# Reading order, weight interleaving and start addresses of the gate and up matmuls in a hybrid decoder layer

## The chip, the cores and the metric

The kernel runs on one core of a Trainium2 chip. The metric is device time in microseconds, from the first to the last instruction of one execution with what the launch adds around it. The engines are named as in the profile: PE is TensorE's matmuls, PEld its weight loads, DVE is VectorE, ACT is ScalarE, POOL is GpSimd, SP is SyncE. "Pitch" or "spacing" of matmuls means the distance between the starts of two that follow each other.

## The reference

One decoder layer on 512 tokens of width 2048 with 16 learned meta tokens ahead of them, all in float32:

```python
n = rmsnorm(h, g_mix)
q, k, v, gb, gc, u = split(n @ w_in)          # attention: 8 heads x 128; convolution: 1024 channels
o_attn = stick_breaking_attention(norm(q), norm(k), v)
o_conv = gb * causal_dwconv(gc * u, conv_w)
h = h + concat(rmsnorm(o_attn), rmsnorm(o_conv)) @ w_out
n2 = rmsnorm(h, g_ffn)
h = h + (silu(n2 @ w_gate) * (n2 @ w_up)) @ w_down    # hidden width 5632
return h[:, 16:]
```

The change touches only the two products `n2 @ w_gate` and `n2 @ w_up`.

## The kernel before, in words

**Number format.** Each float32 operand is held as a high part, rounded to the matmul's own format (fp32r), and a low part, the rest. A product takes three matmuls: high x high, high x low, low x high. Each of them loads a 128x128 block of weights and moves 256 columns (tokens) past it.

**Blocks and pairs.** The FFN works on pairs. Gate and up of one hidden tile f (128 of the 5632 hidden units, so there are FT = 44 tiles) form one pair: two matrices of 2048 x 128, each cut in two quarters of 1024 rows, against activations cut in two halves of the rows and two halves of the tokens. By a scheme with seven products in place of eight (`pair_product`, L900 to 945) the pair is computed from seven `block_product`s (L871 to 891). Each takes one sum of weight quarters and one sum of activation blocks, and accumulates into one of three banks of PSUM, x, y or z. A block product of gate and up has 8 blocks of 128 rows and three matmuls for each, so 24 matmuls, and a pair has 168.

**Weights.** A quarter is 128 partitions x 1024 columns of float32, and comes in by one transfer from `w_gu` (`load_quad`, L168, on SP's queue). On the host (L1388) the quarter is laid out so that its 8 blocks of 128 columns lie side by side in a partition; block k is columns 128k to 128k+127. DVE adds quarters (`add_quads`, L213, and L278), ACT makes the high part (L203), DVE the low part (L206) in one of three places of `sw_split`, ahead of TensorE by two block products (`prepare`, L235; `next_w`, L304, keeps the distance). The pieces go in the order of the list `pieces` (L145 to 150); `pairs[i]` with CONV <= i < CONV + FT are the gate and up pairs.

**Activations.** The seven activation blocks f0 to f6 stay in SBUF for all 44 pairs. Each is a tile of 128 partitions with a high and a low part, of 8 row blocks and 256 tokens each. `slots` (L1017) makes them: it asks for 64 elements more than it needs and starts the block 4 elements (16 bytes) into the tile. In the allocation of this kernel each of these tiles begins at 224 modulo 256 bytes, so every block begins at 240, and as its parts and row blocks are multiples of 1024 bytes, so does every moving operand. The same helper makes the `ring` and `first` tiles of the down projection, which begin at 240 too. Blocks f3, f0, f1, f2, f5 are allocated at L1028, f6 and f4 at L1094 to 1096; f4 and f6 are loaded back from DRAM, the others are written by `split_f` (L1116) in the output projection.

**The matmul itself.** In `block_product` the slice `kk` (L885) picks 128 neighbouring columns of the weights, `ah` and `al` are 256 neighbouring tokens, and `p` 256 neighbouring columns of the bank. The three matmuls are L887 (high x high), L890 (high x low) and L891 (low x high). The convolution's pairs go through the same lines with activations from the tiles `n` and `mixed`, whose blocks begin at other places, and the down projection with those of `first` and `ring`.

**Around it.** After a pair DVE and ACT scale, apply silu, multiply gate and up and split the result (`gate`, L1217); POOL stores it to DRAM (L1206), from where the down projection loads it.

Of the kernel before, what the change touches and what calls it, by code (L numbers as in the profile page):

```python
# [10 lines left out]
F32R = mybir.dt.float32r  # L11
# [4 lines left out]
P = 128  # L16
# [7 lines left out]
FT = FF // P  # L24
# [3 lines left out]
EPS = 1e-6  # L28

Q0 = [0, 112, 240, 368, 496]  # L30


@with_exitstack
def hybrid_layer(ctx: ExitStack, tc: tile.TileContext, xT, w_in, w_out, w_gu, w_down, vecs, out):
# [10 lines left out]
    ve, sc, gp, pe = nc.vector, nc.scalar, nc.gpsimd, nc.tensor  # L45

    def open_pool(name, bufs=1, **kw):
        return tc.alloc_tile_pool(name=name, bufs=bufs, reuse_waits="tile", **kw)
# [17 lines left out]
    def small(name):  # L66
        return sm.tile([P, 512], F32, tag="sm", name=name)
# [56 lines left out]
    CONV = len(pairs)  # L124

    def gate_up(f):
        return 8, [w_gu[n, f, k] for k in range(2) for n in range(2)]
# [261 lines left out]
    ms, r, eps_r2, r2 = accs[1], rpool.tile([P, L], F32, name="r"), accs[1], acc  # L389
# [95 lines left out]
    def host(m, name):  # L485
        return mpool.tile([P, 8 * N + (48 if m == 0 else 0)], F32R, tag=f"m{m}", name=name)
# [3 lines left out]
    for t, row in zip(hosts, ((("kh", 384), ("kl", 384), ("sh", L), ("sl", L)), (("qh", SEQ), ("ql", SEQ), ("bh", 288), ("bl", 288)))):  # L490
        at = 0
# [129 lines left out]
    def attend(h, kn, kh, kl, qn, qh, ql, v):  # L621
# [4 lines left out]
        for b in (2, 1, 0):  # L626
            zs[b] = z = small(f"z{h}_{b}")
            kk, q0 = slice(b * P, (b + 1) * P), Q0[b]
            n = SEQ - q0
# [23 lines left out]
        for s in (2, 1, 0):  # L653
# [21 lines left out]
            else:  # L675
                gp.memset(lw[0:1, a : a + Q0[s + 1] - Q0[s]], 0.0)

        def sums(s):
# [11 lines left out]
            if s:  # L690

                n, (a0, b0) = SEQ - Q0[s], SEG[s - 1]
                th, tl = hl[s - 1]
# [19 lines left out]
        def mix(ws):  # L713
            o = small(f"o{h}")
            for b in range(3):
                kk, q0 = slice(b * P, (b + 1) * P), Q0[b]
                th, tl = ws[b]
                pe.matmul(o[:, q0:], vh[:, kk], th, start=b == 0, stop=False)
                pe.matmul(o[:, q0:], vh[:, kk], tl, start=False, stop=False)
                pe.matmul(o[:, q0:], vl[:, kk], th, start=False, stop=False)  # L720
            pe.matmul(o[:, Q0[3] :], v32[:, :P], lw[:, 1184:1328], start=False, stop=False)
            pe.matmul(o[:, Q0[4] :], v32[:16, P:], lw[:16, 1328:1344], start=False, stop=True)
            g = g_att[:, h : h + 1]
# [147 lines left out]
    def block_product(ps, act, start):  # L871

        hi, lo = next_w()
        i = pieces[used[0] - 1][1]
        m = max(1, ps.shape[-1] // T2)
        cols = ps.shape[-1] // m  # L880
        n = pairs[i][0] // m
        for j in range(m):
            p, skip = ps[:, j * cols : (j + 1) * cols], m > 1 or not start
            for k in range(n):
                kk = slice((j * n + k) * P, (j * n + k + 1) * P)  # L885
                ah, al = act(0, k), act(1, k)
                opening = pe.matmul(p, hi[:, kk], ah, start=start and j == k == 0, stop=False, skip_group_check=skip)  # L887
                if j == k == 0:
                    tc.keep_in_program_order(opening)
                pe.matmul(p, hi[:, kk], al, start=False, stop=False, skip_group_check=skip)  # L890
                pe.matmul(p, lo[:, kk], ah, start=False, stop=k == n - 1, skip_group_check=skip)  # L891

    between, side_read = [], [None]

# [100 lines left out]
    for m in range(2):  # L995
        t = host(m, f"oa{m}")[:, : 4 * SEQ].rearrange("p (h a b) -> p h a b", h=2, a=2)
# [17 lines left out]
    fpool = open_pool("fpool", side="right")  # L1014
    hbuf = open_pool("hbuf", side="right")

    def slots(pool, dt, m, n, name, tail=60, **kw):  # L1017

        c = 2 * m * n * T2
        t = pool.tile([P, 4 + c + tail], dt, name=name, **kw)  # L1020
        t = t[:, 4 : 4 + c].rearrange("p (s a k t) -> p s a k t", s=m, a=2, k=n)
        return [t[:, s] for s in range(m)]

    def slot(pool, dt, n, tag, name):
        return slots(pool, dt, 1, n, name, tag=tag)[0]

    acts = {}
    for i in (3, 0, 1, 2, 5):  # L1028
        acts[i] = slot(fpool, F32R, 8, f"f{i}", f"f{i}")
    pad(fpool, 160)  # L1030
    fx = {i: dram.tile([P, 2, 8, T2], F32R, name=f"fx{i}") for i in (4, 6)}
    def wide_tmp(tag, dt=F32, bufs=1):
# [29 lines left out]
    for i, j in enumerate(OUT_TILES):  # L1062
        hj = wide_tmp("h", bufs=2)
        gp.dma_start(hj, xT[j][:, META:])
        if 0 < i < KT - 1:
            out_tile()
            for part in range(2):
                wide_product(ps_out[i + 1][part], (oa, oc)[part])
        if i == KT - 2:

            oapool.release()
            ocpool.release()
            mpool.release()
            fp = open_pool("fp")
            pad(fp, 64)
            sides = fp.tile([P, 3 * T2], F32, name="sides")
            rings_p = {0: open_pool("ring_0")}
            pad(rings_p[0], 32)
            rings, n_ring, ring = {}, [6], {}

            groups = {0: (0, 1), 1: (1, 2), 3: (1, 1), 4: (1, 1), 5: (1, 1), 6: (2, 1), 7: (2, 5)}

            def new_places(i):
                p, m = groups[i]
                for n, t in enumerate(slots(rings_p[p], F32R, m, 6, f"ring{i}", tag=f"ring{i}")):
                    ring[i + n] = t

            def ring_place():
                n_ring[0] += 1
                return ring[(n_ring[0] - 1) % 12]  # L1090

            new_places(0)
            fpool_last = open_pool("fpool_last")
            acts[6] = slot(fpool_last, F32R, 8, "f6", "f6")  # L1094
            pad(fpool_last, 1024)
            acts[4] = slots(fpool_last, F32R, 1, 8, "f4", tail=0)[0]
            with tc.high_priority(1 << 20):
                load_f(4, 7)
        ps = ps_out[i]
        half, k = divmod(j, 8)  # L1100
        if half == 1:

            src = hbuf.tile([P, 6, T2], F32, tag="src", name=f"src{k}")

        def residual(eng):
            ve.tensor_tensor(t1, ps[0][0][0], acc_a, ALU.mult)
            eng.tensor_tensor(hj, hj, t1, ALU.add)
            for o, a, b in ps[1]:
                ve.tensor_tensor(t2[:, a:b], o, acc_c[:, a:b], ALU.mult)
                eng.tensor_tensor(hj[:, a:b], hj[:, a:b], t2[:, a:b], ALU.add)  # L1110
                blks = src[:, 2 * half + a // T2 : 2 * half + b // T2]
                sc.activation(blks, hj[:, a:b].rearrange("p (a t) -> p a t", t=T2), AF.Copy, scale=g_ffn[:, j : j + 1])
                if a:
                    late_block()

        def split_f(s, i):  # L1116
            split(acts[s][:, 0, k], acts[s][:, 1, k], src[:, i])

        def late_block():
            ve.tensor_tensor(src[:, 4], src[:, 3], src[:, 1], ALU.subtract)  # L1120
            split_f(1, 4)

        def third_block():
            ve.scalar_tensor_tensor(src[:, 4], src[:, 4], -1.0, src[:, 0], ALU.mult, ALU.subtract)
            split_f(2, 4)

        def fourth_block():
            ve.scalar_tensor_tensor(src[:, 5], src[:, 4], -1.0, src[:, 2], ALU.mult, ALU.subtract)
            if i < KT - 1:
                ve.tensor_tensor(src[:, 1], src[:, 0], src[:, 1], ALU.subtract)  # L1130
            split_f(3, 5)

        def fifth_block():
            ve.tensor_tensor(src[:, 1], src[:, 0], src[:, 1], ALU.subtract)
            split_f(4, 1)
            square_sum(acc_h, hj, False, wide_tmp("h", bufs=2), ve)
            hbuf.release()
            nonlocal apool
            apool = open_pool("apool")

        if i == KT - 1:
            with tc.high_priority(1 << 20):
                residual(ve)
                split_f(0, 0)
            between.extend([third_block, fourth_block, fifth_block])
        else:
            residual(gp if half else ve)
            if half:
                split_f(5, 2)
            else:  # L1150
                split_f(0, 0)
                late_block()
                third_block()
                fourth_block()
            st = two(wide_tmp("st", F32R, 2))
            split(st[:, 0], st[:, 1], src[:, 3 if half else 1])
            gp.dma_start(fx[6 if half else 4][:, :, k], st)
            if i == KT - 2:
                with tc.high_priority(1 << 20):
                    load_f(6, 8)  # L1160
        if i < KT - 1:
            square_sum(acc_h, hj, i == 0, t1)
        (gp if i < KT - 1 else nc.sync).dma_start(out[j], hj)
    assert not waiting
    acts = [acts[s] for s in range(7)]
# [31 lines left out]
    at = [(c, k) for c, n in enumerate(CHUNKS) for k in range(n)]  # L1197
# [56 lines left out]
    for f in range(FT):  # L1254
# [11 lines left out]
        x = ffn_pair(acts, g1, u1, (h_scale, h_scale_rest)[f] if f < 2 else None, hook if f > AT_ONCE - 4 else None)  # L1266
# [52 lines left out]
    for j in range(KT // 4):  # L1319
# [3 lines left out]
        x = ffn_pair([rings[0, s] for s in range(7)], c1, c2)  # L1323
# [90 lines left out]
```

## Time and profile before

| | us |
|---|---|
| median of the runs shown (2027.21 and 2027.36) | 2027.28 |
| span of the profiled execution, first to last instruction | 2025.8 |
| PE busy in the span | 2019.7 |
| DVE busy | 1723.3 |
| ACT busy | 1077.9 |
| gate and up, 764.08 to 1603.08 of the span | 839.00 |
| down projection, 1603.08 to 2021.84 | 418.76 |
| convolution pairs, 385.44 to 587.73 | 202.29 |

The profiled execution is known by its span; the runs' median lies 1.5 us above it, which is taken for what lies around the span. The profile's page lists the busy time of each engine, the granted clock of TensorE in forty slices, the chain of work that ended last, and groups of instructions by line. A matmul's duration there runs from its start to its modelled end in the pipeline, and overlaps the next: what counts is the distance between starts, which the timeline gives.

### The profile page before, as it was taken

The numbers are of one execution on the slowest core, as the hardware profiler recorded it, in microseconds if no ns is written. First come the engines' busy times: TensorE is split into PE (matmuls) and PEld (weight loads), VectorE is DVE, ScalarE is ACT, GpSimd is POOL, SyncE is SP. The second block draws the span as 40 slices with busy tenths as digits, with TensorE's granted clock in tenths as the row PEclk, the third lists the DMA queues.
The fourth block names the chain that finished last, engine by engine and source line by source line (L and its number), as shares of the span: only waits on it lengthen the run. The fifth ranks groups of instructions, "written<-read, shape, count | busy, mean of one in ns | idle before, by whom it ended". The sixth has DMA issues, their size and how long they took to land.

```text
span 2025.8 us, 39704 instructions
## 1 busy us (share of the span) xinstructions
PE 2019.7 (100%) x16158; PEld 1961.8 (97%) x16158; DVE 1723.3 (85%) x2199; ACT 1077.9 (53%) x1559; POOL 337.3 (17%) x507
## 2 busy tenths in 40 slices
PE   9999999999999999999999999999999999999999
PEld 8999999999998889999999999999999999999999
DVE  7877777698877778999988988988988978888888
ACT  7876676444454445555555555555555544444443
POOL 0111111200014440111110110110110243131211
PEclk9999999999999999999999999999999999999999
DMA  6333343833255555556554554554554999797864
GB/s 222 116 135 115 125 136 136 282 105 110 99 198 179 165 161 194 171 153 186 173 160 148 167 164 149 164 166 151 162 166 151 290 339 352 170 318 193 222 149 91
DMA packets 156664, 356.31 MB, mean 176 GB/s; under 512 B 13696, under 2 KB 68224, under 8 KB 155712
## 3 DMA queue, kind: packets, MB, share of 16 engines
q1 hardware_dynamic: 72640, 216.73, 32.2%
q0 software_dynamic: 83696, 136.99, 25.0%
q8 instruction: 127, 2.08, 0.4%
q14 instruction: 57, 0.47, 0.1%
q10 hardware_dynamic: 144, 0.04, 0.0%
HBM read 275.78 MB, written 77.92 MB: 175 GB/s over the span
## 4 chain that ended last, share of the span: by engine, by line
PE 99%; DMA 0%; DVE 0%; SPq 0%; ACT 0%; issue 0%
PE x L887 14%; PE x L891 14%; PE x L890 14%; PE z L887 7%; PE z L890 7%; PE z L891 7%; PE y L891 3%; PE y L887 3%; PE y L890 3%; PE pk L342 3%; PE pv L342 3%; PE pq L342 3%; PE pv L340 2%; PE pk L340 2%; PE pq L340 1%; PE pb L342 1%
## 5 line engine op out<-in xcount | busy, mean ns | idle before, releaser
L203 ACT CAST sw_split<-sw_in 128x1024 fp32r<-128x1024 f32 (+3 forms) x671 | 662.4, 989 | 708.7 <-PE x L890 174.2
L206 DVE TENSOR_TENSOR sw_split<-sw_in,sw_split 128x1024 fp32r<-128x1024 f32 (+3 forms) x671 | 775.5, 1156 | 140.4 <-ACT sw_split L203 133.0
L887 PE MATMUL x<-f,sw_split 128*128 128x256 f32 x1408 | 387.5, 275 | 0.1
L891 PE MATMUL x<-f,sw_split 128*128 128x256 f32 x1408 | 387.2, 275 | 0.0
L890 PE MATMUL x<-f,sw_split 128*128 128x256 f32 x1408 | 387.2, 275 | 0.0
L887 PEld LDWEIGHTS x<-f,sw_split 128*128 128x128 f32 x1408 | 264.3, 188 | 0.7 <-DVE u L937 0.5
L890 PEld LDWEIGHTS x<-f,sw_split 128*128 128x128 f32 x1408 | 264.3, 188 | 0.0
L891 PEld LDWEIGHTS x<-f,sw_split 128*128 128x128 f32 x1408 | 264.3, 188 | 0.0
L1206 POOL DMA_DIRECT2D fd<-s x147 | 103.7, 921 | 708.0 <-DVE s L353 632.1
L887 PE MATMUL z<-f,sw_split 128*128 128x256 f32 x704 | 193.6, 275 | 0.0
L890 PE MATMUL z<-f,sw_split 128*128 128x256 f32 x704 | 193.6, 275 | 0.0
L891 PE MATMUL z<-f,sw_split 128*128 128x256 f32 x704 | 193.6, 275 | 0.0
L216 DVE TENSOR_TENSOR sw_in<-sw_in 128x1024 f32<-128x1024 f32 (+1 forms) x164 | 187.7, 1145 | 5.4 <-DMA sw_in<-w_in 0.8
L887 PE MATMUL x<-ring,sw_split 128*128 128x256 f32 x608 | 167.2, 275 | 0.0
L890 PE MATMUL x<-ring,sw_split 128*128 128x256 f32 x608 | 167.2, 275 | 0.0
L891 PE MATMUL x<-ring,sw_split 128*128 128x256 f32 x608 | 167.2, 275 | 0.0
L890 PEld LDWEIGHTS z<-f,sw_split 128*128 128x128 f32 x704 | 132.2, 188 | 0.0
L891 PEld LDWEIGHTS z<-f,sw_split 128*128 128x128 f32 x704 | 132.2, 188 | 0.0
L887 PEld LDWEIGHTS z<-f,sw_split 128*128 128x128 f32 x704 | 132.2, 188 | 0.0
L887 PEld LDWEIGHTS x<-ring,sw_split 128*128 128x128 f32 x608 | 114.1, 188 | 0.0
L891 PEld LDWEIGHTS x<-ring,sw_split 128*128 128x128 f32 x608 | 114.1, 188 | 0.0
L890 PEld LDWEIGHTS x<-ring,sw_split 128*128 128x128 f32 x608 | 114.1, 188 | 0.0
(701 smaller groups left out, 5276.9 us busy)
## 6 DMA issues: line engine op xcount, KB each, us to landing
sw_in<-w_gu SPq DMA_DIRECT2D x176, 512.0 KB, 3.8
sw_in<-w_in SPq DMA_DIRECT2D x90, 512.0 KB, 3.3
fd<-s POOLq DMA_DIRECT2D x147, 256.0 KB, 5.1
sw_in<-w_down SPq DMA_DIRECT2D x96, 384.0 KB, 4.2
ring<-fd POOLq DMA_DIRECT2D x42, 768.0 KB, 17.6
sw_in<-w_out SPq DMA_DIRECT2D x32, 512.0 KB, 3.3
out_T<-d POOLq DMA_DIRECT2D x54, 256.0 KB, 4.6
mix_dram<-st_x POOLq DMA_DIRECT2D x16, 516.0 KB, 4.1
```

What stands on the lines that cost most here:

```text
L203: cast[0] = sc.copy(hi, src)
L206: latest[0] = ve.tensor_tensor(lo, src, hi.bitcast(F32), ALU.subtract)
L216: return ve.tensor_tensor(sums[name], a, b, ALU.add)
L340: pe.matmul(ps, wh, ah[:, a:b], start=k + i == 0, stop=False)
L342: pe.matmul(ps, w, x[:, a:b], start=False, stop=k + i == last and x is (al if used[0] <= n_first else ah))
L887: opening = pe.matmul(p, hi[:, kk], ah, start=start and j == k == 0, stop=False, skip_group_check=skip)
L890: pe.matmul(p, hi[:, kk], al, start=False, stop=False, skip_group_check=skip)
L891: pe.matmul(p, lo[:, kk], ah, start=False, stop=k == n - 1, skip_group_check=skip)
L1206: gp.dma_start(fd[c][s][:, :, k], t[:, :, i])
```

## The change

Three things change, all for the gate and up pairs alone.

- A list `WALKS` of 44 entries gives each pair one of 11 orders of the moving columns and one of 4 interleavings of the weights. All 44 combinations occur once, in the order of the list: four pairs with one order and the interleavings 1, 2, 4, 8, then the next order.
- `walk` reorders the 256 columns of the moving operand and of the PSUM output in the same way, so each result lands in its old place. "n" is the old order and "r" the reverse. "b4" to "b8" go first through all columns whose byte address, counted from the block's start, has a 0 in that bit, and then through those with a 1: "b4" takes 16 bytes, skips 16, and so on; "b8" takes 256 bytes and skips 256. "t6" to "t9" take 16 bytes of each stretch of 64, 128, 256 or 512 bytes, then the next 16 bytes of each.
- With interleaving s the columns of s neighbouring weight blocks are dealt out in turn, so the 128 weights of one block lie 4s bytes apart, and s blocks share s x 512 bytes. The host lays `w_gu` out in that way.
- The blocks of activations begin at other places: `slots` takes the start as an argument. In bytes modulo 256 the blocks 0 to 6 begin at 240, 0, 192, 128, 240, 64 and 16, where all began at 240. The tiles' sizes and places stay.

```diff
+WALKS = [(m, w) for m in ("n", "r", "b4", "b5", "b6", "b7", "b8", "t6", "t7", "t8", "t9") for w in (1, 2, 4, 8)]
+
+def walk(t, how):
+    if how == "n":
+        return t
+    if how == "r":
+        return t[:, ::-1]
+    n = 1 << int(how[1:]) - 2
+    if how[0] == "b":
+        return t.rearrange("p (m b i) -> p b m i", b=2, i=n)
+    return t.rearrange("p (m g i) -> p g m i", g=n // 4, i=4)
...
         n = pairs[i][0] // m
+        hm, hw = WALKS[i - CONV] if CONV <= i < CONV + FT else ("n", 1)
         for j in range(m):
-            p, skip = ps[:, j * cols : (j + 1) * cols], m > 1 or not start
+            p, skip = walk(ps[:, j * cols : (j + 1) * cols], hm), m > 1 or not start
             for k in range(n):
-                kk = slice((j * n + k) * P, (j * n + k + 1) * P)
-                ah, al = act(0, k), act(1, k)
-                opening = pe.matmul(p, hi[:, kk], ah, start=start and j == k == 0, stop=False, skip_group_check=skip)
+                wh, wl = (w.rearrange("p (g c s) -> p g s c", c=P, s=hw)[:, (j * n + k) // hw, k % hw] for w in (hi, lo))
+                ah, al = (walk(act(x, k), hm) for x in range(2))
+                opening = pe.matmul(p, wh, ah, start=start and j == k == 0, stop=False, skip_group_check=skip)
...
-                pe.matmul(p, hi[:, kk], al, start=False, stop=False, skip_group_check=skip)
-                pe.matmul(p, lo[:, kk], ah, start=False, stop=k == n - 1, skip_group_check=skip)
+                pe.matmul(p, wh, al, start=False, stop=False, skip_group_check=skip)
+                pe.matmul(p, wl, ah, start=False, stop=k == n - 1, skip_group_check=skip)
...
-        t = t[:, 4 : 4 + c].rearrange("p (s a k t) -> p s a k t", s=m, a=2, k=n)
+        t = t[:, at : at + c].rearrange("p (s a k t) -> p s a k t", s=m, a=2, k=n)
...
-        acts[i] = slot(fpool, F32R, 8, f"f{i}", f"f{i}")
+        acts[i] = slot(fpool, F32R, 8, f"f{i}", f"f{i}", {0: 4, 1: 8, 2: 56, 3: 40, 5: 24}[i])
...
-            acts[6] = slot(fpool_last, F32R, 8, "f6", "f6")
+            acts[6] = slot(fpool_last, F32R, 8, "f6", "f6", 12)
...
+    def gate_up(w):
+        t = tiles(w, 1024)
+        for f, (_, s) in enumerate(WALKS):
+            t[f] = t[f].reshape(2, P, 8 // s, s, P).swapaxes(3, 4).reshape(t[f].shape)
+        return t
...
-        "w_gu": np.stack([tiles(a("w_gate")[0], 1024), tiles(a("w_up")[0], 1024)]),
+        "w_gu": np.stack([gate_up(a("w_gate")[0]), gate_up(a("w_up")[0])]),
```

More of the change, by code (lines that the diff above doesn't have):

```diff
@@ L1015, in hybrid_layer, with slots, slot @@
     hbuf = open_pool("hbuf", side="right")
-    def slots(pool, dt, m, n, name, tail=60, **kw):
+    def slots(pool, dt, m, n, name, tail=60, at=4, **kw):
         c = 2 * m * n * T2
         t = pool.tile([P, 4 + c + tail], dt, name=name, **kw)
-        t = t[:, 4 : 4 + c].rearrange("p (s a k t) -> p s a k t", s=m, a=2, k=n)
+        t = t[:, at : at + c].rearrange("p (s a k t) -> p s a k t", s=m, a=2, k=n)
         return [t[:, s] for s in range(m)]
-    def slot(pool, dt, n, tag, name):
-        return slots(pool, dt, 1, n, name, tag=tag)[0]
+    def slot(pool, dt, n, tag, name, at=4):
+        return slots(pool, dt, 1, n, name, tag=tag, at=at)[0]
     acts = {}
     for i in (3, 0, 1, 2, 5):
-        acts[i] = slot(fpool, F32R, 8, f"f{i}", f"f{i}")
+        acts[i] = slot(fpool, F32R, 8, f"f{i}", f"f{i}", {0: 4, 1: 8, 2: 56, 3: 40, 5: 24}[i])
     pad(fpool, 160)
```

## The prediction

> **What bounds the kernel now.** I read the page from the top: the busy line of the engines, the granted clock, the chain that ended last.
>
> ```profile
> span 2025.8 us, 39704 instructions
> PE 2019.7 (100%) x16158; PEld 1961.8 (97%) x16158; DVE 1723.3 (85%) x2199; ACT 1077.9 (53%) x1559; POOL 337.3 (17%) x507
> ...
> PEclk9999999999999999999999999999999999999999
> ...
> PE 99%; DMA 0%; DVE 0%; SPq 0%; ACT 0%; issue 0%
> ```
>
> TensorE works from end to end at the full granted clock, and 99% of the chain is its own matmuls, each behind the one before. Nothing else sets the time. The table of busy time by stretch places the change: gate and up, the convolution pairs, and (second view) gate and up cut to the instructions that touch the tiles f.
>
> ```profile
> 764.08:1603.08 839.00, 838.90 (x7397) 838.28 (x7396) 757.60 (x855) 442.68 (x581) 115.11 (x163) 1.00 0.55 168
> 385.44:587.73 202.29, 202.14 (x1683) 201.68 (x1682) 175.17 (x200) 97.95 (x128) 5.67 (x10) 1.00 0.41 139
> ```
> ```profile
> 764.08:1603.08 839.00, 838.44 (x7392) 838.01 (x7392) 2.02 (x5) 2.01 (x5) 1.42 (x2) 1.00 0.55 168
> ```
>
> The columns are length, then busy time and count of PE, PEld (weight loads), DVE, ACT, POOL, then granted clock, DMA share, GB/s. Gate and up is 44 pairs x 7 block products x 8 blocks x 3 matmuls = 7392 matmuls, 41% of the span: 839.00 / 7392 = **113.5 ns from one matmul to the next**. The mean of 275 ns that a matmul shows in the list of groups is its length in the pipeline, not its price; the price is the distance between starts. DVE is busy 757.6 of 839 us, but it waits for TensorE, not the reverse. So the change is worth 7392 times whatever it does to that distance: one nanosecond is 7.4 us, and 2% of the time (40.5 us, about what a measurement of this kernel can tell from no change) is 5.5 ns.
>
> The distance can be read in the timeline. Three stretches of the same kind of matmul (256 columns, fp32r, a new 128x128 weight each): in gate and up, in the last gate pair of the convolution on the x blocks, and right after it on the y blocks.
>
> ```profile
> 999.80 0.28 PE L891 MATMUL x<-f,sw_split 128*128 128x256 f32 x1
> ...
> 1007.96 0.28 PE L891 MATMUL y<-f,sw_split 128*128 128x256 f32 x1
> ```
> ```profile
> 458.51 0.29 PE L887 MATMUL x<-n,sw_split 128*128 128x256 f32 x1
> ...
> 461.05 0.29 PE L891 MATMUL x<-n,sw_split 128*128 128x256 f32 x1
> ...
> 461.53 0.28 PE L887 MATMUL y<-n,sw_split 128*128 128x256 f32 x1
> ...
> 462.01 0.28 PE L890 MATMUL y<-n,sw_split 128*128 128x256 f32 x1
> ```
>
> First: 72 steps in 8.16 us, 113.3 ns. Second: 20 steps in 2.54 us, **127 ns**. Third: 4 steps in 0.48 us, **120 ns**. Shape, type, clock and weight layout are the same; what differs is where the moving block begins. By the addresses of the kernel's allocation every f block begins 240 bytes past a multiple of 256, every x<-n block there at 136, every y<-n block at 128, and the weights always at 128. The convolution's mixed blocks begin at all multiples of 8. Over that whole stage the second row above gives 202.29 / 1683 = 120.2 ns, for 257.4 columns on average (70% have 258), so 119.5 ns for 256. So the places of the two streams that TensorE reads together, moving columns and next weights, change its pace between 113.3 and 127 ns, and gate and up sits at the good end.
>
> How much room the weight load has, the attention shows, where a matmul of only 16 columns leaves the loads to follow each other (timeline of the weight loads):
>
> ```profile
> 59.36 0.19 PEld L630 LDWEIGHTS z<-host,host 128*128 128x128 f32 x1
> 59.47 0.19 PEld L631 LDWEIGHTS z<-host,host 128*128 128x128 f32 x1
> ```
>
> Back to back they start 0.11 us apart. So a load occupies about 110 of the 113.3 ns: it is hidden, with some 3 ns to spare, and any slower load would show in full.
>
> [...]
>
> **The change part by part.** *Instructions, bytes, queues:* none is added, removed or moved. 7392 matmuls, 7392 weight loads, the 176 weight transfers (below) and all splits keep count and size; the new weight order is made on the host, and the adds and splits of DVE and ACT treat a 1024-column quarter element by element. They lie under TensorE, 757.6 and 442.7 us busy in 839, and a slower TensorE gives them more time. Without that cover the DVE work would set the end; here it comes 81 us short of doing so.
>
> ```profile
> sw_in<-w_gu SPq DMA_DIRECT2D x176, 512.0 KB, 3.8
> ```
>
> *Starts:* the seven blocks of activations, formerly all at 240, begin (in the order 0 to 6) at 240, 0, 192, 128, 240, 64, 16. Each serves one seventh of the matmuls, so five sevenths (5280) leave the good place. At the convolution's average that costs 119.5 - 113.5 = 6.0 ns each, 5280 x 6.0 = 32 us. Ends: 0 and 127 - 113.5 = 13.5 ns, 71 us.
>
> *Order of the moving columns:* ten of eleven orders are new, each for the same columns of input and output. All but the reversal keep four neighbours (16 bytes) together and then jump. Every matmul of the trace reads straight on, so no row prices a jump. From below: a gain down to the load's pace, 110 ns. From above: the slowest pace a place gave, 127 ns, taken as what a bad meeting of the streams costs. Blocks 0 and 4, which stay at 240, lose by it too: their good meeting belongs to the straight order.
>
> *Interleaving:* of the 44 pairs 11 keep weights side by side; 33 read them 8, 16 or 32 bytes apart, so a load sweeps 1, 2 or 4 KB instead of 512 bytes, in as many reads. It is unpriced as well. From below: no change of the load and so again 110 ns. From above: a load that takes double, 220 ns.
>
> *The sum.* I take the three parts as one: they all decide how the two streams meet. For a quarter of the pairs (weights side by side) the convolution's average, +6.0 ns. For three quarters the middle between that average and the worst steady row, (119.5 + 127) / 2 = 123.2 ns, +9.7 ns, since a load that sweeps further meets the moving stream oftener. Mean 0.25 x 6.0 + 0.75 x 9.7 = 8.8 ns, x 7392 = **65 us**. Span 2025.8 + 65 = 2090.8; the median of the runs (2027.28) lies 1.5 us over the span, so **2092 us**. The down projection keeps its order and places and its 113.3 ns.
>
> **The rivals.**
> 1. *Price by reads* (2149 us): the convolution's +6.0 ns belongs to loads that sweep 512 bytes; at steps of 2, 4 and 8 the load touches two, four and four times as many 16-byte pieces. If meetings grow so, +6, +12, +24, +24 ns, mean 16.5, x 7392 = 122 us. For: pace depends on places at all. Against: 127 ns is the worst steady row.
> 2. *The load becomes the bound* (2421 us): at steps of 4 and 8 every weight lies in a piece of its own. If that halves the load's pace, 22 pairs (3696 matmuls) go from 113.5 to 220 ns: +394 us. For: only 3 ns to spare. Against: a load takes 0.86 ns per weight now, far slower than a moving column's 0.44 ns, so it may be paced by something other than its reads. [...]
> 3. *Starts alone count* (2059 us): the orders within a block and the load's steps are smoothed out by whatever TensorE fetches at a time; then only the 32 us of the five moved starts remain. For: the starts are the only thing with a row. That would also mean that the change does not do what it says to the reading.
> 4. *The streams are kept apart* (the other side, 2001 us at best): a step of 2 makes the load advance at the moving stream's own pace in bytes, so the two need never meet, and several orders may do the same. Then the load's 110 ns is the floor: 3.5 x 7392 = 26 us less. It decides only where the mean of all pairs falls below 113.5 ns; with a quarter of the pairs gaining and the rest unchanged it is 2021. For: 113.3 sits above the load's pace, so something still costs. Against: the good place was a single one, and the new starts and orders are spread widely.
>
> **How the numbers follow.** Chances: the sum 0.45, rival 1 0.18, rival 2 0.10, rival 3 0.13, rival 4 with all that ends near or below the old time 0.14. The sum's own range is 2060 to 2125 (spacings of 118 to 127 ns). The whole range leaves out rival 2 (0.10) and the better part of rival 4 (0.10): **2027 to 2240**, whose top holds rival 1 and a load slowed by half of rival 2's price (197 us, 2224). 2% is a spacing of 119.0 ns. Within 2% are rival 3, nearly all of rival 4 and a low end of the sum (0.03): 0.29; faster by more would need 108 ns, under the load's pace: 0.01; slower 0.70.
>
> **What would show it.** Right: all of the growth in the stretch of gate and up (some 904 us), unequal from pair to pair by spacing, the convolution and the down projection as before to a microsecond, TensorE still 99% of the chain, the clock at full. Within a pair the spacing should change with the block product, since the seven blocks have their own places. Rival 1: spacing rises with the step, 1 < 2 < 4. Rival 2: pairs of steps 4 and 8 near 0.22 us per matmul whatever the order. Rival 3: two neighbouring pairs alike, only products differ. Rival 4: many pairs at 110 to 113 ns. Wrong altogether: a wait of TensorE on DVE, ACT or a transfer that was not there before, or growth outside gate and up.

## The result and the profile after

The changed kernel takes **2519.66 us** (two runs, 2519.23 and 2520.09) against 2027.28: the ratio is 1.243, with an interval of 1.239 to 1.247. The forecast was 2092 with a range up to 2240. The sign was right and the size was missed by 428 us. First the lines of the changed kernel's page that answer to those of before: span, busy engines, clock, chain.

```profile
span 2518.3 us, 39735 instructions
...
PE 2512.6 (100%) x16158; PEld 2455.1 (97%) x16158; DVE 1742.4 (69%) x2199; ACT 1074.6 (43%) x1559; POOL 337.6 (13%) x507
...
PEclk9999999999999999999999999999999999999999
...
PE 99%; DMA 0%; DVE 0%; SPq 0%; ACT 0%; issue 0%
```

The counts of matmuls and weight loads are the same, the clock is full, and TensorE's own matmuls are still 99% of the chain. TensorE waits for nothing new. Every matmul stands behind the one before it, and some have become slower. The table of busy time by stretch shows which (length; busy time and count of PE, PEld, DVE, ACT, POOL; clock; DMA share; GB/s): the part before gate and up, gate and up, and the rest.

```profile
0.00:764.49 764.49, 762.55 (x5069) 705.66 (x5070) 600.45 (x877) 438.51 (x694) 132.82 (x238) 1.00 0.46 152
764.49:2095.34 1330.85, 1330.79 (x7396) 1330.36 (x7395) 777.04 (x855) 439.05 (x580) 115.11 (x163) 1.00 0.36 109
2095.34:2518.30 422.96, 419.22 (x3698) 419.02 (x3697) 364.88 (x468) 197.04 (x285) 89.65 (x106) 1.00 0.82 225
```

The first part took 764.08 before and the last 2025.8 - 1603.08 = 422.72, so 0.4 and 0.2 us are all that they changed. Gate and up went from 839.00 to 1330.85, which is 491.85 of the 492.4 us. The mean spacing there is 1330.85 / 7392 = 180.0 ns, where it was 113.5. The same table cut by pairs, TensorE alone (length, busy time and count, clock, DMA share, GB/s), shows what the mean is made of. The first fence has the four pairs of the reversed order with the interleavings 1, 2, 4, 8, the second those of the order t8 with 1 and 4.

```profile
885.15:905.20 20.05, 20.05 (x170) 1.00 0.40 132
905.20:925.03 19.83, 19.83 (x170) 1.00 0.59 173
925.03:964.24 39.21, 39.21 (x171) 1.00 0.21 68
964.24:1004.99 40.75, 40.75 (x170) 1.00 0.27 84
```
```profile
1846.26:1868.94 22.68, 22.68 (x169) 1.00 0.51 151
...
1892.13:1931.63 39.50, 39.50 (x170) 1.00 0.29 87
```

A pair starts 168 matmuls (the counts take in one to three that were still running at its start). So 20.05 us is a spacing of 119.3 ns, and 39.21 and 40.75 us are 233.4 and 242.6. The order t8 costs 135.0 ns at step 1, but at step 4 its pair is as long as any other: 235.1. Over all eleven orders the pairs of step 4 lie between 233 and 236 ns and those of step 8 between 240 and 243. The means by step are 120.9 (the first pair taken without a wait before its seventh product, which the kernel before has too), 122.8, 234.9 and 241.3 ns. Hence the bill: the 3696 matmuls of steps 4 and 8 cost (238.1 - 113.5) x 3696 = 460 us, and the 3696 of steps 1 and 2 cost (121.85 - 113.5) x 3696 = 31 us. The slow matmuls follow each other evenly, as the timeline of a step 8 pair shows: from the first line to the last are five matmuls in 1.20 us, 240 ns each, with nothing else between them.

```profile
999.70 0.41 PE L907 MATMUL x<-f,sw_split 128*128 128x256 f32 x1
...
1000.90 0.40 PE L906 MATMUL x<-f,sw_split 128*128 128x256 f32 x1
```

### The profile page after: what moved, and what is told of

The parts are those of the page before. It is cut to its first block, busy times and chain, and to the rows that moved or that the text cites. A ratio compares the mean times of both kernels' runs of the same rounds, so it can differ in the third digit from the quotient of the medians.

```text
span 2518.3 us, 39735 instructions
## 1 busy us (share of the span) xinstructions
PE 2512.6 (100%) x16158; PEld 2455.1 (97%) x16158; DVE 1742.4 (69%) x2199; ACT 1074.6 (43%) x1559; POOL 337.6 (13%) x507
## 4 chain that ended last, share of the span: by engine, by line
PE 99%; DMA 0%; DVE 0%; SPq 0%; ACT 0%; issue 0%
PE x L903 15%; PE x L907 15%; PE x L906 15%; PE z L906 7%; PE z L903 7%; PE z L907 7%; PE y L906 4%; PE y L903 4%; PE y L907 4%; PE pk L357 2%; PE pv L357 2%; PE pq L357 2%; PE pv L355 1%; PE pk L355 1%; PE pq L355 1%; PE pb L357 1%
## 5 line engine op out<-in xcount | busy, mean ns | idle before, releaser
L903 PE MATMUL x<-f,sw_split 128*128 128x256 f32 x1408 | 483.4, 343 | 0.1
L906 PE MATMUL x<-f,sw_split 128*128 128x256 f32 x1408 | 483.4, 343 | 0.0
L907 PE MATMUL x<-f,sw_split 128*128 128x256 f32 x1408 | 483.2, 343 | 0.0
L903 PEld LDWEIGHTS x<-f,sw_split 128*128 128x128 f32 x1408 | 371.3, 264 | 0.5 <-DVE u L953 0.5
L906 PEld LDWEIGHTS x<-f,sw_split 128*128 128x128 f32 x1408 | 371.5, 264 | 0.0
L907 PEld LDWEIGHTS x<-f,sw_split 128*128 128x128 f32 x1408 | 371.5, 264 | 0.0
L903 PE MATMUL z<-f,sw_split 128*128 128x256 f32 x704 | 241.9, 344 | 0.0
L906 PE MATMUL z<-f,sw_split 128*128 128x256 f32 x704 | 241.9, 344 | 0.0
L907 PE MATMUL z<-f,sw_split 128*128 128x256 f32 x704 | 241.8, 344 | 0.0
L906 PEld LDWEIGHTS z<-f,sw_split 128*128 128x128 f32 x704 | 185.8, 264 | 0.0
L907 PEld LDWEIGHTS z<-f,sw_split 128*128 128x128 f32 x704 | 185.8, 264 | 0.0
L903 PEld LDWEIGHTS z<-f,sw_split 128*128 128x128 f32 x704 | 185.7, 264 | 0.0
L906 PE MATMUL y<-f,sw_split 128*128 128x256 f32 x352 | 121.0, 344 | 0.0
L903 PE MATMUL y<-f,sw_split 128*128 128x256 f32 x352 | 121.0, 344 | 0.0
L907 PE MATMUL y<-f,sw_split 128*128 128x256 f32 x352 | 120.9, 344 | 0.0
```

Source lines behind the costliest of these rows:

```text
L903: opening = pe.matmul(p, wh, ah, start=start and j == k == 0, stop=False, skip_group_check=skip)
L906: pe.matmul(p, wh, al, start=False, stop=False, skip_group_check=skip)
L907: pe.matmul(p, wl, ah, start=False, stop=k == n - 1, skip_group_check=skip)
```

## The experiments

The pattern (growth by step and not by order) is rival 2's: the load of the next weights has become the bound. That leaves open why a load of the same 128 weights takes twice as long. **Theory A**: the weights are fetched in aligned pieces of 16 bytes (the spacing stops growing where each weight has a piece of its own: 122.8, 234.9 and 241.3 ns at steps 2, 4 and 8), a piece takes some 1.8 ns to open (by estimate 234.9 / 128), and a load at steps of 4 or more opens 128 of them in place of 32. Its rivals: **B**, certain strides collide in SBUF (powers of two bad, odd steps good); **C**, the two streams hinder each other, so that orders and starts share in the price and it is added to a matmul of any length; **D**, the price follows the length that a load sweeps. Times are of one run each; the kernel before on the same chips gave 2027.45 to 2028.24; "spacing" is a pair's length over 168.

**Orders and starts alone.** All weights side by side:

```diff
-WALKS = [(m, w) for m in ("n", "r", "b4", "b5", "b6", "b7", "b8", "t6", "t7", "t8", "t9") for w in (1, 2, 4, 8)]
+WALKS = [(m, w) for m in ("n", "r", "b4", "b5", "b6", "b7", "b8", "t6", "t7", "t8", "t9") for w in (1, 1, 1, 1)]
```

> The changed kernel with all 44 interleavings set to 1; orders and starts stay. Theory A (a weight load pays for every 16-byte piece that it opens, and with one weight to a piece it takes about twice as long): the steps of 4 and 8 carry nearly all of the loss; the pairs with step 1 in the changed kernel's trace have a mean spacing of 120.9 ns, so 7392 x (120.9 - 113.5) = 55 us over the kernel before, 2082 us. Rival C (orders and starts make load and moving stream meet, and the steps only multiply the meetings): the pairs now at step 1 keep a part of the loss that their neighbours in the list brought about, above 2150 us.

Measured: 2083.12 us, 55.6 more than before. The stretch of gate and up, cut to the tiles f, gives 885 / 7318 = 120.9 ns:

```profile
764.00:1649.00 885.00, 884.48 (x7318) 884.28 (x7319) 1.97 (x5) 1.61 (x4) 1.42 (x2) 1.00 0.52 156
```

The orders keep the spacings that they have in the changed kernel's step 1 pairs: t8 135.6, t9 127.5, t6 115.7. This fits A, and not C, in which orders and starts carry much of the price.

**Interleavings alone.** Straight order and old starts:

```diff
+WALKS = [("n", w) for _ in range(11) for w in (1, 2, 4, 8)]
...
-        acts[i] = slot(fpool, F32R, 8, f"f{i}", f"f{i}", {0: 4, 1: 8, 2: 56, 3: 40, 5: 24}[i])
+        acts[i] = slot(fpool, F32R, 8, f"f{i}", f"f{i}", 4)
...
-            acts[6] = slot(fpool_last, F32R, 8, "f6", "f6", 12)
+            acts[6] = slot(fpool_last, F32R, 8, "f6", "f6")
```

> The interleavings 1, 2, 4, 8 in turn over the 44 pairs, with straight order and all starts at 240 as before. Theory A: steps 4 and 8 at 235 and 241 ns as in the changed kernel, step 1 at 113.3, step 2 between 113 and 120: 11 x 168 x (0 + 3 + 121.5 + 127.5) ns = 466 us more, about 2493 us. Rival C (the load loses its time in meetings with the moving stream, which order and start decide): with the good start and the straight order steps 4 and 8 come well under 200 ns, below 2350 us in all.

Measured: 2501.81 us, 474.3 more. Four neighbouring pairs, steps 1, 2, 4, 8:

```profile
883.99:903.03 19.04, 19.04 (x169) 1.00 0.44 131
903.03:923.19 20.16, 20.16 (x170) 1.00 0.63 174
923.19:962.95 39.76, 39.76 (x171) 1.00 0.22 69
962.95:1003.32 40.37, 40.37 (x169) 1.00 0.28 85
```

Spacings of 113.3, 120.0, 236.7 and 240.3 ns. The interleaving alone makes 96% of the growth. The two halves add up to 474.3 + 55.6 = 530, 38 more than the whole change costs. That is cover: under a load of 238 ns the orders and starts cost nothing on average, which takes away half of their 55.6 (27.8), and at step 2 they add only 122.8 - 120.0 = 2.8 ns instead of 7.4, which takes away another 4.6 x 1848 = 8.5 us (1848 matmuls have step 2). Together 36 of the 38.

**What of a step makes a load slow.** Straight order, old starts, weights on the host as before. Eleven patterns of a load in turn, among them odd steps and steps that begin half a piece or a quarter of a piece later. It reads other weights than the reference's.

```diff
+LOADS = (("1", 0), ("1", 2), ("2", 0), ("2", 1), ("3", 0), ("4", 0), ("4", 2), ("5", 0), ("6", 0), ("7", 0), ("8", 0)) * 4
+def load_view(w, how, k):
+    s, off = int(how[0]), how[1]
+    at = min(k * 128, (1024 - 128 * s) // 64 * 64 - (64 if off else 0)) + off
+    return w[:, at : at + 127 * s + 1 : s]
...
```

> Gate and up read their weights at eleven patterns in turn, four pairs each: steps 1 to 8, and steps 1, 2 and 4 from another start within 16 bytes (8, 4 and 8 bytes on). Order and starts as before. The steps are taken from the old layout, so gate and up use wrong weights. Theory A (16-byte pieces): steps 1 and 2 at 113 to 121 ns; step 3 (96 pieces for 128 weights) between, about 175; steps 4, 5, 6, 7 and 8 all alike, 232 to 243; the start within the piece changes nothing at steps 1, 2 and 4. Rival B (the load collides with itself where its step is a multiple of 16 bytes, because it keeps to few banks): steps 3, 5 and 7 stay below 150 ns, 6 in between, only 4 and 8 at 235 and more. Rival D (the length of the sweep counts): a steady rise over 1 to 8.

Measured: 2565.6 us. Pairs of steps 1, 1 begun 8 bytes later, 2, 3, 4, 4 begun 8 bytes later, 5 and 8:

```profile
1108.84:1127.92 19.08, 19.08 (x169) 1.00 0.38 112
1127.92:1147.89 19.97, 19.97 (x170) 1.00 0.58 169
1147.89:1168.06 20.17, 20.17 (x171) 1.00 0.52 158
...
1188.21:1217.34 29.13, 29.13 (x170) 1.00 0.33 105
1217.34:1257.10 39.76, 39.76 (x170) 1.00 0.30 86
1257.10:1296.86 39.76, 39.76 (x169) 1.00 0.21 67
1296.86:1334.67 37.81, 37.81 (x169) 1.00 0.33 91
...
1412.22:1452.92 40.70, 40.70 (x170) 1.00 0.21 65
```

In ns: 113.6, 118.9, 120.1, **173.4**, 236.7, 236.7, 225.1, 242.3. Step 3 sweeps 1536 bytes, 96 pieces: 1.81 ns each. Step 4 sweeps 128 pieces: 1.85 ns. From there on every weight has a piece of its own, and steps 5 to 8 cost no more in kind (225 to 242). Step 3 between, and step 5 nearly as dear as 4, speak against B; step 8 with twice the sweep of 4 at nearly the same price speaks against D. Two things were not as expected. Steps 5 and 6 (225.1 and 226.6 ns) lie below the 232 to 243 forecast, and what the 17 ns between step 5 and step 8 come from is open. And at step 1 the start within a piece does matter: 8 bytes later it costs 118.9 ns against 113.6, which the count of pieces (33 in place of 32) doesn't explain; at step 4 it changes nothing.

**A longer matmul over the same load.** The kernel before, with only the weights of the output projection at step 4. There 744 of the 792 matmuls have 512 columns; the last 48 have 256.

```diff
-                kk = slice(k * P, (k + 1) * P)
-                pe.matmul(ps, hi[:, kk], ah[:, a:b], start=n == 0, stop=False)
+                wh, wl = (w.rearrange("p (g c s) -> p g s c", c=P, s=4)[:, k // 4, k % 4] for w in (hi, lo))
+                pe.matmul(ps, wh, ah[:, a:b], start=n == 0, stop=False)
...
```

> The kernel before with the weights of the output projection interleaved by 4 and laid out for it, so that its matmuls of 512 columns (about 227 ns apart) load at step 4; gate and up as before. Theory A with a load that takes some 220 to 235 ns by itself: it is nearly hidden under 512 columns, the 768 matmuls go to 230 to 245 ns, and the whole to 2030 to 2042 us. Rival C (a load at step 4 takes time away from the moving stream): it adds its 120 ns here too, 92 us, 2119 us.

Measured: 2037.96 us against 2027.49. The same 70 us of the output projection, first in the kernel before, then here:

```profile
620.00:690.00 70.00, 70.00 (x308) 1.00 0.51 166
```
```profile
620.00:690.00 70.00, 70.00 (x299) 1.00 0.52 159
```

Less the two that were still running at the start, 70 us over 306 is 229 ns and over 297 is 236: 7 ns more, where gate and up moved by 120. The last 48 matmuls, with 256 columns, go from 119.0 to 231.0 ns in the same two traces, though order and starts are as before. So each kind makes about half of the 10.5 us, 744 x 7 ns and 48 x 112 ns. The load is not a surcharge but a floor at about 236 ns, just above what 512 columns take themselves. C falls.

**Starts alone.**

```diff
+WALKS = [("n", 1)] * 44
```

> The changed kernel with straight order and step 1 in all pairs: the new starts alone. The four straight pairs of the run with all steps 1 had 117.1 to 118.0 ns; if nothing but the starts matters there, all 44 pairs have some 117.2 ns and the kernel 7392 x 3.7 = 27 us more, 2055 us. By the forecast's term (five of seven blocks at the convolution's 119.5 ns) it is 2059 us, and products of blocks 0 and 4, at 240, have 113.3 ns from their first matmul on. If matmuls carry their meeting over to the next product, these two products begin above 113.3 and come down within the product.

Measured: 2055.74 us, 28.1 more. By block product, 0 to 6, the spacings are 115.4, 118.4, 117.6, 120.1, 115.8, 113.6 and 119.1 ns, for starts at 240, 0, 192, 128, 240, 64 and 16. The two at 240 are dearer than before because each follows a product at a worse place: their first eleven or so matmuls go at 114 to 122 ns before they fall in at 113. The orders are the rest of the first experiment, 55.6 - 28.1 = 27.5 us.

**Which part of an order costs.** Weights side by side, old starts; moving columns and output columns are walked by different orders (s: every second, fourth or eighth column in turn; q: the same with pairs of columns). The results land in other columns than the reference's.

```diff
+MOVES = (("n", "n"), ("t8", "n"), ("n", "t8"), ("t9", "n"), ("n", "t9"), ("s2", "n"), ("s4", "n"), ("s8", "n"), ("n", "q2"), ("n", "q8"), ("q4", "n")) * 4
...
+    if how[0] == "s":
+        return t.rearrange("p (m i) -> p i m", i=n)
+    if how[0] == "q":
+        return t.rearrange("p (m g i) -> p g m i", g=n, i=2)
```

> Gate and up with the order of the moving columns and that of the output set apart, eleven combinations in turn, four pairs each; starts at 240, weights side by side. Since the two orders differ, the tokens of gate and up come out in other places. Orders: t8 and t9 as in the change; s2, s4, s8 take every 2nd, 4th or 8th column in sweeps; q2, q4, q8 take 8 bytes of each stretch of 16, 32 or 64 bytes. If the price of t8 (135 ns) and t9 (128) lies on the reading side, t8 and t9 on the moving operand alone cost 130 to 140 and 124 to 130, and on the output alone 113 to 116; if it lies in PSUM the other way round. If the moving stream pays for 16-byte pieces as the weight load does: s2 at 113 to 122 ns, s4 and s8 about doubled, 220 to 240, and q4, which opens each piece twice, 113 to 122. If it has enough fetched ahead, s4 and s8 stay under 150. Output in pieces of 8 bytes (q2, q8): no change, 113 to 116, if PSUM only wants pairs; 200 and more if every jump costs.

Measured: 2360.35 us. Pairs of (moving, output) = n/n, t8/n, n/t8; then s2/n, s4/n, s8/n; then n/q8, q4/n:

```profile
1057.55:1076.64 19.09, 19.09 (x169) 1.00 0.36 109
1076.64:1099.26 22.62, 22.62 (x171) 1.00 0.55 159
1099.26:1118.37 19.11, 19.11 (x170) 1.00 0.51 153
...
1158.75:1197.19 38.44, 38.44 (x171) 1.00 0.34 93
1197.19:1236.39 39.20, 39.20 (x170) 1.00 0.23 68
1236.39:1272.98 36.59, 36.59 (x170) 1.00 0.34 94
...
1292.09:1311.13 19.04, 19.04 (x171) 1.00 0.52 140
1311.13:1350.31 39.18, 39.18 (x171) 1.00 0.27 90
```

The whole price of an order is on the reading side: t8 on the moving columns costs 134.6 ns, t8 on the output 113.8, and jumps between pairs of output columns (q8) 113.3. The second finding was a miss: I had put s2 and q4 at 113 to 122, and they take 228.8 and 233.2. Two columns of a piece in a row are not enough for the moving stream: with one or two it runs at about half its pace, 217.8 to 233.3 ns against 113.3 (three were not tried). For s2 and q4 my count was wrong, too: they open each of the 64 pieces twice, and 128 openings in 228.8 and 233.2 ns are 1.79 and 1.82 ns each, theory A's own price. What that price does not fit is s4 and s8, which open a piece for each of the 256 columns: they should take some 460 ns and take 233.3 and 217.8. Every order of the change keeps four columns together, and all of them stay at 115 to 135 ns. Why t8 and t9 cost 134.6 and 126.7 ns all the same is not shown.

**Which starts are good.** Straight order, weights side by side; a pair's blocks begin at one of 44 places (sixteen 16 bytes apart, then those 8 bytes on, then twelve 4 bytes on). Reads other activations than the reference's.

```diff
+SHIFTS = [4 * j for j in range(16)] + [4 * j + 2 for j in range(16)] + [4 * j + 1 for j in range(0, 12)]
...
+                return t.rearrange("p a k t -> p (a k t)")[:, (part * 8 + min(k, 6)) * T2 + shift :][:, :T2] if shift else t[:, part, k]
```

> Gate and up with straight order and step 1, all seven blocks of a pair read from one place, another in each pair: 240 + 16j modulo 256 for j = 0 to 15, then these 8 bytes on, then twelve of them 4 bytes on. The activations are read shifted, so gate and up use wrong ones. If what counts is how load and moving stream meet: multiples of 16 between 113.3 and 122 ns, several as good as 240, 128 at 120 as in the convolution; 8 bytes on between 114 and 127 with 136 at 126.7; 4 bytes on no better than those. Rival: 240 is the only good place. No place under 112.5 if the load's own pace (some 110 ns) is the floor.

Measured: 2074.17 us. Pairs with starts at 0, 64, 128, 192 and 136 modulo 256:

```profile
783.79:803.72 19.93, 19.93 (x171) 1.00 0.49 159
...
863.38:882.45 19.07, 19.07 (x170) 1.00 0.63 171
...
942.04:962.18 20.14, 20.14 (x170) 1.00 0.63 173
...
1021.61:1041.39 19.78, 19.78 (x170) 1.00 0.53 162
...
1263.57:1283.31 19.74, 19.74 (x171) 1.00 0.50 153
```

Spacings of 118.6, 113.5, 119.9, 117.7 and 117.5 ns. Of the 16 places on a piece's border two are good, 240 (113.3 in the kernel before) and 64 (113.5); the other 14 cost 116.7 to 120.0. The places 8 bytes on cost 117.5 to 121.5 ns, those 4 bytes on 120.2 to 123.3. So 240 is not unique, and none goes below 113.3. The 136 that went at 127 ns in the convolution, and was expected to do so here, goes at 117.5, so a place has no fixed price.

**The load with the moving stream out of its way.** The eleven patterns of loads again, with 64 columns in the last seven of a product's eight row blocks; three quarters of those columns' work is left out.

```diff
+                if CONV <= i < CONV + FT and k:
+                    ah, al, q = ah[:, :64], al[:, :64], p[:, :64]
```

> The eleven load patterns of the run on load steps again, but of each block product only the first row block moves 256 columns; the other seven move 64, so that there the loads follow each other with little beside them. Gate and up lose three quarters of most products and use wrong weights. It measures the load's own time. Theory A (the load opens one 16-byte piece per 1.8 ns and takes 0.86 ns per weight at least): 110 to 113 ns at steps 1 and 2, about 170 at step 3, and 215 to 240 at steps 4 to 8, as with the full 256 columns. Rival C (the moving stream makes the load slow): steps 4 to 8 come well below, to 110 to 150 ns, since the moving stream is idle three quarters of the time. The 6.6 ns that step 2 costs under 256 columns (120.0 against 113.4) should vanish here, if it is a meeting of the two streams.

Measured: 2830.01 us, and a surprise. The granted clock along the span, two matmuls of the first such stretch (18 steps apart), and pairs of steps 1, 3, 4 and 8:

```profile
PEclk9999999999955555555555555555555555999999
```
```profile
764.57 0.28 PE L904 MATMUL y<-f,sw_split 128*128 128x64 f32 x1
...
766.58 0.28 PE L904 MATMUL y<-f,sw_split 128*128 128x64 f32 x1
```
```profile
1168.02:1203.85 35.83, 35.83 (x169) 0.50 0.24 74
...
1311.37:1347.21 35.84, 35.84 (x169) 0.50 0.23 74
1347.21:1386.49 39.28, 39.28 (x169) 0.50 0.32 87
...
1539.55:1579.59 40.04, 40.04 (x169) 0.50 0.21 66
```

At the full clock the load of neighbouring weights alone takes 2.01 / 18 = 111.7 ns. Within the first pair the clock falls to half (0.56 on average from 770 to 800 us, 0.50 from 800 on) and stays there to the end of gate and up. Steps 1, 2 and 3 then all take 213 ns, so that the half clock hides what this run was to show of steps 2 and 3, while 4 and 8 take 233.8 and 238.3, about as at the full clock (236.7 and 242.3). So there are two paces in a load: one for each weight, which goes with TensorE's clock (111.7 ns at the full clock, 213 at half), and one for each piece, which does not (236.7 and 233.8 ns at step 4). Why the two differ is not shown.

**The same with 192 columns**, to keep the clock up:

```diff
-                    ah, al, q = ah[:, :64], al[:, :64], p[:, :64]
+                    ah, al, q = ah[:, :192], al[:, :192], p[:, :192]
```

> As the run with 64 moved columns, but with 192 in seven of eight row blocks, which with 64 had let the granted clock fall to half. 192 columns take some 85 ns, less than a load, so at full clock the spacing is the load's own time. Gate and up lose a quarter of most products and use wrong weights. Theory A: step 1 at 111 to 113 ns, steps 4 to 8 at 222 to 242 as before, with 64, 192 or 256 columns. Step 2: 111 to 114 ns if the 6.6 ns that it costs under 256 columns is a meeting of the two streams, 118 to 120 if it belongs to the load. Step 3: 165 to 175 ns (with 64 columns it was hidden under the half clock's 213).

Measured: 2620.41 us. The clock still fell, but not everywhere. Pairs of steps 1 and 2 are now so short that TensorE waits for the splits of the weights between products (busy 20.75 of 23.45 us in the first pair of step 2), so step 2 is read inside a product: two matmuls, 18 steps apart and at the full clock. Below them are whole pairs of steps 3 and 4:

```profile
810.84 0.28 PE L904 MATMUL z<-f,sw_split 128*128 128x192 f32 x1
...
812.98 0.28 PE L904 MATMUL z<-f,sw_split 128*128 128x192 f32 x1
```
```profile
852.25:881.38 29.13, 29.13 (x170) 1.00 0.29 91
881.38:921.03 39.65, 39.65 (x170) 0.55 0.34 100
```

Step 2 takes 2.14 / 18 = 118.9 ns under 192 columns too, and 119.6 to 119.8 over longer stretches. Had its 120 been a meeting with 256 moving columns, it would have come down to 111 to 114; it did not. The 120 belongs to the load, 64 pieces at 1.87 ns, as far as a run with 192 moving columns can tell. Steps 3 and 4 are as with 256 columns, 173.4 and 236.0.

## Why the prediction was right and wrong, step by step

**Right: what bounds, and where.** All of the growth is in gate and up, the parts around it stayed within half a microsecond, TensorE is 99% of the chain at the full clock, and DVE, ACT and the transfers are hidden (DVE 777 of 1331 us). That the load had hardly any room was right as well: some 3 ns were read, off a single gap of 0.11 us, and 113.3 - 111.7 = 1.6 measured.

**Right in size, with some luck: the starts.** 32 us were forecast and 28.1 measured, but the 32 charged all five moved blocks alike and the two at 240 nothing. One of the five, at 64, costs nothing, and the two at 240 pay some 2 ns each for what comes before them. **Right in size: steps 1 and 2.** For step 1 the sum had +6.0 ns and +7.4 came, about half from starts and half from orders. For step 2 it had +9.7 and +9.3 came, which is luck: the sum priced meetings of the two streams, while 6.5 of the 9.3 are the load's own time (120.0 ns alone) and only 2.8 come from orders and starts. The worst row for a meeting, 127 ns, was too low for the order t8 (135), but it is one of eleven.

**Wrong: the interleaving at steps 4 and 8.** This is the step that failed: "I take the three parts as one: they all decide how the two streams meet", and with it "For three quarters the middle between that average and the worst steady row", +9.7 ns. The runs showed that the interleaving is no matter of meeting: it makes the load itself longer than the matmul that should hide it, with straight order and good starts too (e2: 236.7 and 240.3 ns). In the change steps 4 and 8 cost +124.6. The difference, 114.9 x 3696 = 425 us, is all but 3 us of the miss. The load's upper end of 220 ns stood beside it, and I chose by rows of the other stream, which price a bad meeting and say nothing of a load. Rival 2 had the mechanism and the 22 pairs, at a chance of 0.10. Its price was short by (238.1 - 220) x 3696 = 67 us, and without the 31 us of steps 1 and 2 it came to 2421.

**The argument that talked rival 2 down was a misreading.** It said that 0.86 ns per weight is far slower than 0.44 ns per moving column, so the load may be paced by something other than its reads. True for weights side by side, and the wrong question. What counts is whether the reads become the pace when they grow fourfold. The prediction called the spaced load one of "as many reads"; counted in pieces it has two and four times as many. A first guess at the price of a piece was in the trace: a moving matmul reads 256 columns of 4 bytes, 64 pieces, in 113.3 ns, so 1.77 ns each was the fastest pace at which that trace showed pieces to come. At that pace the 128 pieces of step 4 take 227 ns, step 2's 64 just what the moving stream takes, 113. Measured were 236 and 120. The row alone could not say that pieces set that pace, and s4 and s8 of the moving stream open them faster. Nor did any row of before show that 16 bytes is the size to count by; the run on load steps did (step 3, 96 pieces, 173.4 ns; step 4, 128, 236.7). But an estimate of three lines would have raised rival 2: the load had 3 ns to spare and was to open four times the pieces.

The two streams differ in how many neighbours of a piece they need. For the loads two weights per piece take 120.0 ns and one 236.7, against 113.3 with four. For the moving stream two columns of a piece in a row (s2) already take 228.8 ns, and the orders that keep four together 113.3 to 135.6 with weights side by side.

**Weak: one of the signs.** The spacing does change with the block product, but by little at every step: within a pair by 2 to 6.5 ns at step 1 (the first pair apart), by up to 6.5 at step 4 and by up to 3.4 at step 8. Beside the 120 ns of the load the sign says nothing.

**The other rivals.** Rival 1 (growth of 6, 12, 24, 24 ns) had the right quantity, pieces touched, and took a meeting's price for it; a load opens its pieces whether or not it meets much (233.8 ns at step 4 with 64 moving columns). Rival 3 (starts alone count) is out by e2's 474 us. Rival 4 (streams kept apart at step 2) is out too: 120.0 ns alone, 122.8 in the change, and no place or order below 113.3.

**Open.** Orders s4 and s8 of the moving columns touch a new piece with every column, 256 of them, and take 233 and 218 ns, 0.85 to 0.91 ns per piece. So the 1.8 ns are no law for every stream. All four sparse orders (s2, s4, s8, q4), with one or two neighbours in a row, took 217.8 to 233.3 ns, 0.85 to 0.91 ns per column; why is not shown. Nor is it known why just 240 (113.3 ns) and 64 (113.5) are good starts.

## What to carry to other kernels

When a change spaces out the weights that TensorE loads, count the aligned 16-byte pieces that a load opens before and after, and compare the count times 1.8 ns (here 1.87 at step 2, 1.81 at step 3, 1.85 at step 4) with the time that the load now has. A weight load at steps of four to eight floats took 225 to 242 ns, which even a matmul of 512 columns (229 ns) did not quite hide at step 4. Where a cost has two ends far apart, ask which row belongs to the resource that is asked for more, and not which row is nearest by shape. Output columns could jump in pairs (q2 113.8 ns, q8 113.3); moving columns took, with weights side by side, 113.3 to 135.6 ns with four neighbours and 217.8 to 233.3 with one or two.

## What the runs showed of the hardware that was not expected

- A load has two paces: per weight, tied to TensorE's clock (111.7 ns for 128 at full clock, 213 at half), and per 16-byte piece, not tied to it (233.8 ns for step 4 at half clock, 236.7 at full).
- The granted clock fell to 0.50 in a stream that never stopped, once matmuls moved 64 columns and loads filled the time, and to between 0.50 and 0.72 with 192 columns under loads of steps 4 to 8, though at 1.00 in the pair of step 3 shown above. With 256 columns and the same loads it stayed at 1.00. By an estimate from 113.3 ns for 256 columns, the moving columns filled 47% of the time at step 8 with 256 columns (113 of 242 ns), where the clock stayed, and 38% at step 5 with 192 (85 of 226), where it fell; no run looks between, and what sets the clock is not shown.
- The place of the moving block modulo 256 bytes is worth up to 6% of a matmul (113.3 to 120.0 ns) on a piece's border, with two good places of sixteen, and a product can carry the bad pace of the one before it through its first eleven matmuls (114 to 122 ns at a start of 240, where it then falls in at 113).
